# A seven-product FFN matmul group: four products added in one PSUM tile that a copy seeds, in another order, with its banks in a ring of six

## Chip, cores, metric

The kernel runs on one core of one Trainium2 chip. The metric is the time of one execution in microseconds (us), taken on the device; a kernel's time is the median of several runs. One execution is also profiled; its own time and the span of its trace (first to last instruction) are given beside the median.

## What is computed

A decoder trunk of two layers over 512 tokens of width 1024, all in float32. Each layer is FFN, mixer, FFN, so there are four FFNs; the change is in these alone. The reference, cut to what matters:

```python
D_MODEL = 1024; SEQ = 512; DEPTH = 2; D_FF = 2816

def swiglu(h, w_gate, w_up, w_down):
    return (jax.nn.silu(h @ w_gate) * (h @ w_up)) @ w_down

for i in range(DEPTH):
    x = x + 0.5 * swiglu(rmsnorm(x, ffn1_norm[i]), ffn1_w_gate[i], ffn1_w_up[i], ffn1_w_down[i])
    h = rmsnorm(x, mix_norm[i])
    x = x + (gla_mixer(h, ...) if i % 2 == 0 else sb_mixer(h, ...))
    x = x + 0.5 * swiglu(rmsnorm(x, ffn2_norm[i]), ffn2_w_gate[i], ffn2_w_up[i], ffn2_w_down[i])
return rmsnorm(x, final_norm)
```

## The kernel before, in words

**Tiles and precision.** Activations lie feature-major: tiles of 128 features by 512 tokens. Every float32 operand is cut into a high part `h` and a low part `l` (tile type float32r), and each product is three matmuls, high by high, low by high and high by low. The weights are cut by `Entry.split`: ScalarE (ACT) casts the raw weights to `wh` (L133), VectorE (DVE) subtracts to get `wl` (L134). The raw weights come from DRAM in chunks of 1024 rows by 256 columns (`raw`, two buffers), the down weights in chunks `rawd` of 512 KB. A pair `wh`, `wl` has four buffers, the pair for down weights one, so ACT's cast of down weights has to wait until TensorE (PE) has done with the down product before it.

**The feed.** The work on PE is a queue of entries; each has weights to be cut and a body that issues matmuls. `Feed.start` cuts the weights of up to three entries ahead and loads those of six.

**The seven-product group** (`seven`, the function that is changed). From chunk 3 on for the gate matrix and chunk 2 on for the up matrix, one chunk of 256 columns against the 512 tokens is done as a 2 by 2 block product with seven block products in place of eight (Winograd's form of Strassen's scheme). The weights' blocks are A11, A12, A22 and the sums S1 to S4 of blocks (`sums_12`, `sums_34`, two DVE instructions each); the activations' blocks are `half` (plain) and `t_half` (sums, made once in an FFN). A block product, `prod`, is 4 steps of 3 matmuls of 256 columns, 12 matmuls (L528). Each FFN has 17 such groups, 8 for gate and 9 for up, 68 in all; here they are numbered 0 to 16 in an FFN, the even ones up, the odd ones gate. A group has two entries, `body_1` with four products and `body_2` with three.

The group has three PSUM tiles, `w`, `z` and `q`. Before the change a product that has to be added to several outputs is put in a PSUM region of its own, and the sums are made by DVE outside PSUM: A11 goes to `w` and is copied to an SBUF tile `u2` by ACT (L563); S2 goes to `z`, and DVE adds it to `u2` (L539); S1 goes to `q` and ACT copies it to `c5` (L570); A12 is accumulated in `w`, whose sum is the first output quarter (`left`: a SiLU by ACT, L543, in a gate group, a multiplication by DVE, L545, in an up group). S3 goes to the second half of `z`; DVE adds `u2` and then `c5` (L539, L583). S4 is accumulated in `q`, DVE adds `u2`. A22 goes to the second half of `w`; DVE adds it. `rest` applies SiLU (L549) or the gate (L552), and `close` cuts an up group's result into `hh`, `hl` for the down product.

**The down products** (`down`) stand between the groups. One gives a tile `ps_d`, 12 matmuls of 512 columns (6 in the group of one chunk), and DVE adds it to the residual `x` (L308).

**PSUM.** There are eight banks, under four tags of 2, 3, 2 and 1 buffers; `psum(name)` without a tag takes the next of a ring of eight, for groups, down products and the rest alike.

**What sets the order.** Each engine runs its instructions in the order of its own stream and waits on semaphores. The framework that builds the program lays out each stream and may move an instruction ahead of another one of the code; the built streams are what is shown below.

## Time and profile before

| | us |
|---|---|
| median of 3 runs (lowest to highest) | 1829.39 (1829.24 to 1830.08) |
| the profiled execution | 1829.62 |
| span of its trace | 1827.8 |
| DVE busy | 1454.1 |
| ACT busy | 935.9 |

The profile's page gives the busy time of each engine, the span in 40 slices, the chain of work that ended last and groups of equal instructions with the idle time before them. A timeline row is: start, duration (both us), engine, line, operation, output<-inputs, shape; in brackets the idle time of the engine before it and what ended it. The end of a matmul is modelled, so a product is timed from its first matmul's start to the next product's first. DVE and ACT instructions overlap by some 0.1 us in these rows: the next one may start before the last has ended.

### The profile page before, as it was taken

The page shows a single profiled execution, that of the slowest core. Times are in us where ns is not written, and L with a number is a line of the kernel's source. Part 1 is how long each engine was busy: PE and PEld are TensorE (multiplying, and loading weights), DVE is VectorE, ACT ScalarE, POOL GpSimd, SP SyncE. Part 2 cuts the span into 40 slices and gives each one's busy share as a digit, 9 for nine tenths or more (in the row PEclk, how much of TensorE's full clock was granted, in tenths as well). Part 3 has the DMA queues.
Part 4 walks back from the last instruction along what each step waited for, and adds up shares of the span by engine and source line. Part 5 has one row for each costly group of instructions (what it writes and reads, how often), then busy time and mean ns, then how long its engine had stood idle before and what let it go on. Part 6 is the DMA issues. An engine that isn't in the chain of part 4 may idle for free.

```text
span 1827.8 us, 28865 instructions
## 1 busy us (share of the span) xinstructions
PE 1794.6 (98%) x11790; PEld 1642.5 (90%) x11790; DVE 1454.1 (80%) x2311; ACT 935.9 (51%) x1450; POOL 7.3 (0%) x17
## 2 busy tenths in 40 slices
PE   7999999999999999999999999999999999999998
PEld 6899999889988899999989999999888788999997
DVE  5987878775776988887889878777878769888785
ACT  5544444543664544444464444445888855444344
POOL 0000000100000000000000000000000000000000
PEclk9999999999999999999999999999999999999999
DMA  5333332322123333333234233223222222333321
GB/s 162 101 119 104 106 126 82 113 70 70 47 70 102 107 115 105 104 116 105 81 109 134 86 122 105 92 94 104 70 64 64 67 95 93 127 105 104 117 92 69
DMA packets 177511, 179.01 MB, mean 98 GB/s; under 512 B 4034, under 2 KB 167924, under 8 KB 177380
## 3 DMA queue, kind: packets, MB, share of 16 engines
q1 hardware_dynamic: 176192, 175.13, 29.7%
q8 instruction: 92, 1.51, 0.3%
q0 software_dynamic: 512, 0.99, 0.2%
q10 hardware_dynamic: 676, 1.07, 0.2%
q14 instruction: 39, 0.32, 0.1%
HBM read 175.11 MB, written 2.10 MB: 97 GB/s over the span
## 4 chain that ended last, share of the span: by engine, by line
PE 82%; DVE 10%; ACT 4%; DMA 3%; issue 1%; SPq 0%; ACTq 0%; DVEq 0%
PE ps_d L62 24%; PE ps_w L528 14%; PE ps_f L62 12%; PE ps_z L528 9%; PE ps_q L528 9%; PE ps_t L62 4%; PE ps_b L62 3%; DVE wl L134 2%; PE ps_S L62 1%; DMA raw<-in_ffn_w_up_dram 1%; PE ps_bt L62 1%; ACT wh L133 1%; PE ps_oT L1141 1%; PE ps_z L1079 1%; ACT l L439 1%
## 5 line engine op out<-in xcount | busy, mean ns | idle before, releaser
L134 DVE TENSOR_TENSOR wl<-raw,wh 128x1024 fp32r<-128x1024 f32 x244 | 261.9, 1073 | 68.2 <-ACT wh L133 67.2
L133 ACT CAST wh<-raw 128x1024 fp32r<-128x1024 f32 x244 | 225.4, 927 | 120.9 <-PE ps_f L62 42.0
L62 PE MATMUL ps_d<-hh,wh 128*128 128x512 f32 x672 | 255.0, 379 | 0.0
L62 PE MATMUL ps_d<-hl,wh 128*128 128x512 f32 x672 | 254.8, 379 | 0.0
L62 PE MATMUL ps_d<-hh,wl 128*128 128x512 f32 x672 | 254.8, 379 | 0.0
L133 ACT CAST wh<-s 128x1024 fp32r<-128x1024 f32 x136 | 142.3, 1046 | 131.9 <-PE ps_q L528 76.8
L62 PE MATMUL ps_f<-xh,wh 128*128 128x512 f32 x448 | 177.2, 396 | 5.2 <-ACT wh L133 3.7
L134 DVE TENSOR_TENSOR wl<-s,wh 128x1024 fp32r<-128x1024 f32 x136 | 166.0, 1222 | 17.8 <-ACT wh L133 16.5
L308 DVE SCALAR_TENSOR_TENSOR x<-ps_d,x 128x512 f32<-128x512 f32 x184 | 125.2, 689 | 64.5 <-PE ps_d L62 64.5
L62 PE MATMUL ps_f<-xh,wl 128*128 128x512 f32 x448 | 170.8, 381 | 0.5 <-DVE wl L134 0.5
L62 PE MATMUL ps_f<-xl,wh 128*128 128x512 f32 x448 | 170.5, 381 | 0.0
L133 ACT CAST wh<-rawd 128x1024 fp32r<-128x1024 f32 x84 | 88.0, 1048 | 136.1 <-PE ps_d L62 115.1
L528 PE MATMUL ps_z<-th,wh 128*128 128x256 f32 x544 | 150.2, 276 | 3.1 <-DVE u L539 3.1
L528 PE MATMUL ps_w<-nh,wl 128*128 128x256 f32 x544 | 149.7, 275 | 0.0
L528 PE MATMUL ps_z<-tl,wh 128*128 128x256 f32 x544 | 149.7, 275 | 0.0
L528 PE MATMUL ps_w<-nl,wh 128*128 128x256 f32 x544 | 149.7, 275 | 0.0
L528 PE MATMUL ps_z<-th,wl 128*128 128x256 f32 x544 | 149.7, 275 | 0.0
L528 PE MATMUL ps_w<-nh,wh 128*128 128x256 f32 x544 | 149.6, 275 | 0.0
L62 PEld LDWEIGHTS ps_d<-hl,wh 128*128 128x128 f32 x672 | 127.1, 189 | 17.9
L62 PEld LDWEIGHTS ps_d<-hh,wh 128*128 128x128 f32 x672 | 127.3, 189 | 16.5
L62 PEld LDWEIGHTS ps_d<-hh,wl 128*128 128x128 f32 x672 | 127.3, 189 | 16.4
L134 DVE TENSOR_TENSOR wl<-rawd,wh 128x1024 fp32r<-128x1024 f32 x84 | 102.8, 1224 | 38.3 <-ACT wh L133 38.0
(250 smaller groups left out, 4707.1 us busy)
## 6 DMA issues: line engine op xcount, KB each, us to landing
raw<-in_ffn_w_gate_dram SPq DMA_DIRECT2D x43, 1024.0 KB, 5.2
raw<-in_ffn_w_up_dram SPq DMA_DIRECT2D x43, 1024.0 KB, 5.2
rawd<-in_ffn_w_down_dram SPq DMA_DIRECT2D x84, 512.0 KB, 3.4
raw<-in_gla_w_in_dram SPq DMA_DIRECT2D x12, 1024.0 KB, 5.2
raw<-in_sb_w_in_dram SPq DMA_DIRECT2D x16, 512.0 KB, 3.7
raw<-in_gla_w_out_dram SPq DMA_DIRECT2D x4, 1024.0 KB, 4.9
raw<-in_sb_w_in_dram SPq DMA_DIRECT2D x4, 1024.0 KB, 5.0
raw<-in_sb_w_out_dram SPq DMA_DIRECT2D x4, 1024.0 KB, 4.9
```

Of the source, the lines that this page charges most:

```text
L62: st["pe"] = nc.tensor.matmul(ps, l, r, start=first, stop=last).ins
L133: nc.scalar.copy(h, r).ins,
L134: nc.vector.tensor_tensor(out=l, in0=r, in1=h.bitcast(F32), op=ALU.subtract).ins,
L308: nc.vector.scalar_tensor_tensor(out=x, in0=back_by(ps, 4), scalar=0.5, in1=x, op0=ALU.mult, op1=ALU.add)
L439: st["last"] = nc.scalar.activation(o, i, fn, **kw).ins
L528: nc.tensor.matmul(pairs(o), l_, r_, start=first and j + n == 0, stop=j == 3 and n == 2, skip_group_check=True)
L1079: nc.tensor.matmul(o_, l_, r_, start=first, stop=last, skip_group_check=True)
L1141: nc.tensor.matmul(po[e * 64 : e * 64 + 64, j * P : T], self.v[j][:, c : c + 64], self.wt[p, e][bk][:, c0 : c0 + n], start=j == 0, stop=j ...
```

## The change

In a group, ACT copies A11's result from `w` into `z`, PSUM to PSUM. S2, S3 and A22 are then accumulated onto it in `z`, and between them the running sum is read out: after S2 by an ACT copy to `u2`, after S3 by a DVE addition of `c5` straight into the output tile, after A22 by `left`. The order of the products is A11 S1 S2 A12 S3 S4 A22 (before: A11 S2 S1 A12 S3 S4 A22). In an up group `left` now runs twice on 256 columns in place of one multiplication of 512. The three tiles use the first 256 columns of their banks alone, and the groups take them from a ring of six banks of their own (not the two of tag "a"), while the other PSUM tiles keep their ring of eight, which the groups no longer move on.

```diff
-    turn_ = [0]
+    turn_ = [0, 0]
     def psum(name, tag=None):
-        if tag is None:
+        if tag == "s":
+            tag = "zzztto"[turn_[1] % 6]
+            turn_[1] += 1
+        elif tag is None:
...
             def body_1(W):
-                v["w"], v["z"], v["q"] = psum("ps_w"), psum("ps_z"), psum("ps_q")
-                w, z, q = (v[n][:, 0:H] for n in "wzq")
+                v["w"], v["z"], v["q"] = (psum(n, "s")[:, 0:H] for n in ("ps_w", "ps_z", "ps_q"))
+                w, z, q = (v[n] for n in "wzq")
                 v["o"] = self.tp.tile([P, T], F32, tag="t", name="o0")
                 prod(w, ax, 0, half(0, 0))
-                v["u2"] = part("u2")
-                nc.scalar.copy(v["u2"], w)
-                yield
-                prod(z, s, 4, lambda j: self.t_half(1, j))
-                add(v["u2"], z, v["u2"])
+                nc.scalar.copy(z, w)
                 yield
                 prod(q, s, 0, lambda j: self.t_half(0, j))
                 v["c5"] = part("c5")
                 nc.scalar.copy(v["c5"], q)
                 yield
+                prod(z, s, 4, lambda j: self.t_half(1, j), first=False)
+                v["u2"] = part("u2")
+                nc.scalar.copy(v["u2"], z)
+                yield
                 prod(w, ax, 4, half(4, 0), first=False)
                 left(v["o"], w)
                 yield
             def body_2(W):
-                q, y = v["q"][:, 0:H], v["z"][:, H:T]
+                q, z = v["q"], v["z"]
-                prod(y, s, 0, lambda j: self.t_half(2, j))
-                u3 = o1[:, 0:H]
-                add(u3, y, v["u2"])
-                nc.vector.tensor_tensor(out=o1[:, H:T], in0=u3, in1=v["c5"], op=ALU.add)
+                prod(z, s, 0, lambda j: self.t_half(2, j), first=False)
+                add(o1[:, H:T], z, v["c5"])
                 yield
                 prod(q, s, 4, half(4, 1), first=False)
                 add(o0[:, H:T], q, v["u2"])
                 rest(o0, H)
                 yield
-                o = v["w"][:, H:T]
-                prod(o, a22, 0, lambda j: self.t_half(3, j))
-                add(o1[:, 0:H], o, u3)
-                rest(o1, 0)
+                prod(z, a22, 0, lambda j: self.t_half(3, j), first=False)
+                left(o1, z)
+                rest(o1, H)
                 yield
```

The built streams at three places follow; lines of the changed kernel are 3 higher than before up to L558. The first place is group 6 of the first FFN, an up group, on PE, where product S4 ends and A22 begins. Before:

```order
L528 MATMUL ps_q_1747<-nh_502,wl_1704 128x256
L528 MATMUL ps_q_1747<-nl_503,wh_1703 128x256
L528 MATMUL ps_w_1745<-th_553,wh_1707 128x256 [waits DVE_49]
L528 MATMUL ps_w_1745<-th_553,wl_1708 128x256
L528 MATMUL ps_w_1745<-tl_554,wh_1707 128x256
```

After, at the same place:

```order
L531 MATMUL ps_q_1741<-nh_502,wl_1698 128x256
L531 MATMUL ps_q_1741<-nl_503,wh_1697 128x256
L65 MATMUL ps_d_1871<-hh_839,wh_1733 128x512 [waits DVE_49]
L65 MATMUL ps_d_1871<-hh_839,wl_1734 128x512
L531 MATMUL ps_z_1740<-th_553,wh_1701 128x256 [waits DVE_49]
L531 MATMUL ps_z_1740<-th_553,wl_1702 128x256
L531 MATMUL ps_z_1740<-tl_554,wh_1701 128x256
```

Two matmuls of the down product that follows have moved ahead of A22, and A22 now writes `z`. In a gate group with a down product behind it one matmul has moved; where another group follows at once, two or three of that group's first matmuls have. In 20 of the 68 groups, moreover, the first matmul of the next down product (or group) has moved to between A11 and S1.

The second place is the same group on DVE, from the cut of the next weights (`wl`) to the sums of this group. Before:

```order
L134 TENSOR_TENSOR wl_1804<-raw_1655,wh_1803 128x1024 [waits PE_49,Activation_49]
L545 TENSOR_TENSOR o0_1748<-ps_w_1745,o0_1589 128x256 [waits PE_49]
L134 TENSOR_TENSOR wl_1811<-s12_1807,wh_1810 128x1024 [waits Activation_49]
L539 TENSOR_TENSOR o1_1816<-ps_z_1746,u2_1761 128x256 [waits PE_49]
L539 TENSOR_TENSOR o0_1748<-ps_q_1747,u2_1761 128x256 [waits PE_49]
L583 TENSOR_TENSOR o1_1816<-o1_1816,c5_1788 128x256 [waits DVE_49]
```

After:

```order
L137 TENSOR_TENSOR wl_1798<-raw_1650,wh_1797 128x1024 [waits PE_49,Activation_49]
L548 TENSOR_TENSOR o0_1742<-ps_w_1739,o0_1584 128x256 [waits PE_49]
L137 TENSOR_TENSOR wl_1805<-s12_1801,wh_1804 128x1024 [waits Activation_49]
L542 TENSOR_TENSOR o1_1810<-ps_z_1740,c5_1768 128x256 [waits PE_49]
L542 TENSOR_TENSOR o0_1742<-ps_q_1741,u2_1782 128x256 [waits PE_49]
```

The read of `z` after S3 keeps its place behind the two cuts; of the three additions around it one is gone.

The third place is ACT in group 5 of the first FFN, a gate group, from the cast of the down weights on. Before:

```order
L133 CAST wh_1580<-rawd_1417 128x1024 [waits DMAHW7_49,PE_49,Activation_49]
L563 COPY u2_1602<-ps_w_1586 128x256 [waits PE_49]
L570 COPY c5_1629<-ps_q_1588 128x256 [waits PE_49,Activation_49]
L133 CAST wh_1644<-raw_1488 128x1024 [waits DMAHW0_49,Activation_49]
L543 ACTIVATE o0_1589<-ps_w_1586 128x256 [waits PE_49]
L133 CAST wh_1651<-s12_1648 128x1024
```

After:

```order
L136 CAST wh_1575<-rawd_1413 128x1024 [waits DMAHW7_49,PE_49]
L565 COPY ps_z_1582<-ps_w_1581 128x256 [waits PE_49]
L569 COPY c5_1610<-ps_q_1583 128x256 [waits PE_49,Activation_49]
L573 COPY u2_1624<-ps_z_1582 128x256 [waits PE_49,Activation_49]
L136 CAST wh_1639<-raw_1484 128x1024 [waits DMAHW0_49]
L546 ACTIVATE o0_1584<-ps_w_1581 128x256 [waits PE_49]
L136 CAST wh_1646<-s12_1643 128x1024
```

One copy is added, and the last of the three stands behind the third product (S2) as `c5` stood behind the third product (S1) before; what follows is the same.

## The prediction

> **What bounds the kernel now.** I read the page first, then who waits for whom on PE, then the timeline of two groups.

> ```profile
> span 1827.8 us, 28865 instructions
> PE 1794.6 (98%) x11790; PEld 1642.5 (90%) x11790; DVE 1454.1 (80%) x2311; ACT 935.9 (51%) x1450; POOL 7.3 (0%) x17
> PEclk9999999999999999999999999999999999999999
> ```

> PE is busy for 1794.6 of 1827.8 us, and the change takes no matmul away. So it can only gain what PE idles now. In the view of waits, filtered to PE, the seven-product groups (the rows with `ps_z L528` and `ps_w L528`) have this:

> ```profile
> PE ps_z L528 <- DVE u L539: 3.1, 5, 1.4
> PE ps_w L528 <- DVE o L545: 0.7, 2, 0.3
> ```

> That is 3.8 us in seven waits, all in the first groups of an FFN and in one disturbed by a late load. Nearly all groups run without a gap, which the chain of work that ended last shows for one up group (group 6 of the third FFN):

> ```profile
> 1042.13 1.34 PE ps_z L528 x12
> 1043.47 1.34 PE ps_q L528 x12
> 1044.81 1.34 PE ps_w L528 x12
> 1046.15 5.18 PE ps_d L62 x24
> ```

> A block product takes **1.34 us**, a matmul of a down product 5.18 / 24 = 0.216 us. So a new wait that is covered by one product has 1.34 us in which the other engine must see the end, take its turn, finish and tell PE.

> **What the change saves, and why that is worth little.** Per group three DVE additions go (five before, two now) and an up group gets one more multiplication; ACT gets one copy. By the groups of instructions:

> ```profile
> L539 DVE TENSOR_TENSOR o<-ps_z,u 128x256 f32<-128x256 f32 x68 | 28.5, 419 | 0.0
> L563 ACT COPY u<-ps_w 128x256 f32<-128x256 f32 x68 | 25.3, 372 | 18.5 <-PE ps_w L528 18.5
> L570 ACT COPY c<-ps_q 128x256 f32<-128x256 f32 x68 | 25.3, 372 | 141.6 <-PE ps_q L528 141.6
> L1228 ACT ACTIVATE ps_bt<-x 128x512 f32<-128x512 f32 x8 | 4.8, 602 | 8.2 <-DVE x L1223 8.2
> ```

> DVE loses 68 x 3 x 0.419 - 36 x 0.42 = some 70 us of 1454, ACT gains 68 x 0.372 = 25 us of 936. Neither is the bound, so both count as nothing in themselves: PE's 98% hides them. But the first row matters. The read of `z` after S3 never has idle time before it (0.0 for all 68): DVE always gets to it late, out of a queue. Before the change no matmul waits for that read. After it, **A22 does**, since it accumulates into the same `z`, and only S4 lies between.

> **The new waits, one by one.** In each group PE now waits (1) in S2 for ACT's copy of `w` into `z`, with S1 as cover, (2) in S3 for ACT's copy of `z` to `u2`, with A12 as cover, (3) in A22 for DVE's addition, with S4 and the moved matmuls as cover. The cost of a wait that is not covered comes from one that the trace has (group 1 of the first FFN, DVE's row, then PE's):

> ```profile
> 91.74 0.42 DVE L539 TENSOR_TENSOR u<-ps_z,u 128x256 f32<-128x256 f32 x1
> ...
> 91.56 0.28 PE L528 MATMUL ps_w<-nl,wh 128*128 128x256 f32 x1
> 92.22 0.38 PE L528 MATMUL ps_z<-th,wh 128*128 128x256 f32 x1 [0.39 <-DVE u L539]
> 92.43 0.28 PE L528 MATMUL ps_z<-th,wl 128*128 128x256 f32 x1
> ```

> The addition ended at 92.16; the second matmul came at 92.43, so the first counts as begun one step of 0.11 earlier, at 92.32. PE goes on **0.16 us** after the end of what it waited for.

> (1) and (2): the gate group after the one above, ACT's rows, and the first matmul of its second product:

> ```profile
> 1051.41 1.05 ACT L133 CAST wh<-rawd 128x1024 fp32r<-128x1024 f32 x1 [1.23 <-PE ps_d L62]
> 1052.71 0.37 ACT L563 COPY u<-ps_w 128x256 f32<-128x256 f32 x1 [0.25 <-PE ps_w L528]
> ...
> 1052.51 0.28 PE L528 MATMUL ps_z<-th,wh 128*128 128x256 f32 x1
> ```

> The copy of `w` ends at 1053.08, PE could go on at 1053.24, and S2 as third product is due at 1052.51 + 1.34 = 1053.85: 0.61 us to spare. The copy now goes to PSUM. The trace has no copy from PSUM to PSUM; the nearest rows are ACT's write of 512 columns to PSUM, 602 ns (L1228 above), and 372 ns for 256 columns out of PSUM. Between those ends the copy costs 0.37 to 0.60, and even the upper one leaves 0.38 us. I take 0.37 and no wait. The copy of `z` after S2 stands where that of `c5` stands now and has the same margin. Nothing of length is queued between the three copies on ACT. So (1) and (2) cost nothing.

> (3), the up group. ACT's, DVE's and PE's rows:

> ```profile
> 1040.88 0.37 ACT L570 COPY c<-ps_q 128x256 f32<-128x256 f32 x1 [2.36 <-PE ps_q L528]
> 1041.15 1.05 ACT L133 CAST wh<-raw 128x1024 fp32r<-128x1024 f32 x1
> 1042.17 1.05 ACT L133 CAST wh<-s 128x1024 fp32r<-128x1024 f32 x1
> ...
> 1042.23 1.23 DVE L134 TENSOR_TENSOR wl<-raw,wh 128x1024 fp32r<-128x1024 f32 x1 [0.21 <-ACT wh L133]
> 1043.38 0.42 DVE L545 TENSOR_TENSOR o<-ps_w,o 128x256 f32<-128x256 f32 x1
> 1043.71 1.22 DVE L134 TENSOR_TENSOR wl<-s,wh 128x1024 fp32r<-128x1024 f32 x1
> 1044.84 0.42 DVE L539 TENSOR_TENSOR o<-ps_z,u 128x256 f32<-128x256 f32 x1
> ...
> 1044.65 0.28 PE L528 MATMUL ps_w<-th,wh 128*128 128x256 f32 x1
> ```

> This is a chain: the third product ends, ACT copies, casts, DVE cuts, multiplies, cuts, adds. DVE even waits 0.21 us for ACT at its head, so a DVE with fewer additions doesn't start it sooner, and the order after the change has the same chain with `u2` for `c5`. The addition ends at 1045.26, PE could go on at 1045.42. A22 is due at 1044.65, and with two down matmuls moved ahead of it at 1044.65 + 2 x 0.216 = 1045.08. **0.34 us** are left as a wait.

> (3), the gate group:

> ```profile
> 1055.71 1.05 ACT L133 CAST wh<-raw 128x1024 fp32r<-128x1024 f32 x1
> 1056.73 0.39 ACT L543 ACTIVATE o<-ps_w 128x256 f32<-128x256 f32 x1
> 1057.01 1.04 ACT L133 CAST wh<-s 128x1024 fp32r<-128x1024 f32 x1
> ...
> 1058.12 1.22 DVE L134 TENSOR_TENSOR wl<-s,wh 128x1024 fp32r<-128x1024 f32 x1
> 1059.25 0.42 DVE L539 TENSOR_TENSOR o<-ps_z,u 128x256 f32<-128x256 f32 x1
> ...
> 1059.21 0.28 PE L528 MATMUL ps_w<-th,wh 128*128 128x256 f32 x1
> ```

> The second cut starts 0.07 us after the cast at 1057.01 ends, so here too ACT's chain decides. The addition ends at 1059.67, PE goes on at 1059.83; A22 with one moved matmul is due at 1059.21 + 0.216 = 1059.43: **0.40 us**.

> Behind the waiting A22 on PE stand the rest of the down product and all later groups; DVE's additions to `x` and ACT's cast of down weights wait for those. So each wait moves everything, and since the chain starts anew at each group's third product, it doesn't shrink from group to group.

> Groups 2 to 16 of an FFN are like these two: 4 x 8 = 32 up groups x 0.34 = 10.9 us; 4 x 7 = 28 gate groups x 0.40 = 11.2 us.

> **Groups 0 and 1.** There DVE is behind by more. First and third FFN, DVE's addition and A22 in group 0:

> ```profile
> 86.54 0.42 DVE L539 TENSOR_TENSOR o<-ps_z,u 128x256 f32<-128x256 f32 x1
> 84.97 0.28 PE L528 MATMUL ps_w<-th,wh 128*128 128x256 f32 x1
> ...
> 982.12 0.42 DVE L539 TENSOR_TENSOR o<-ps_z,u 128x256 f32<-128x256 f32 x1
> 981.13 0.38 PE L528 MATMUL ps_w<-th,wh 128*128 128x256 f32 x1 [0.33 <-DVE o L545]
> ```

> First FFN: 86.96 + 0.16 = 87.12 against 84.97 + 3 x 0.11 (three matmuls of group 1 moved ahead) = 85.30, so 1.8 us; I take the same for the second. Third: less the one addition (0.33, the step to the next row on DVE) 82.21 + 0.16 in place of 81.13, so 1.24 later, less the three moved matmuls 0.9; the same in the fourth. Group 1 then waits some 0.4 in each FFN, and what it waits now (about 0.6 in the first two) goes. Sum: 2 x (1.8 + 0.4 - 0.6) + 2 x (0.9 + 0.4) = 5.8 us.

> **The matmuls moved up behind A11** (20 groups) use the cast that ends at 1052.46 above and stand at 1052.51: they wait until 1052.62, 0.11 each, 2.2 us. The bounds are 0 (the cast was early) and the whole cast row, 1.05; the row itself stands nearest.

> **The ring of six.** A group can get a bank that a down product has just left, or the reverse. The tightest is `q` on the bank of the last down tile: that is needed one product after the group's start, and DVE's addition to `x` has long room. I cost it at nothing; with the cover gone it is one DVE row, under 0.7 us, in a quarter of the groups, 12 us at most.

> **Sum.** 10.9 + 11.2 + 5.8 + 2.2 = 30 us on the profiled execution's 1829.62 us (span 1827.8, 1.8 around it; the median shown is 1829.39, 0.2 less): **1859.5 us**.

> **Rivals.**
> *A22 doesn't wait* (not slower). The addition is late because DVE is loaded, and with three additions fewer it comes in time. The point from which this decides: it must end 0.34 (up) and 0.40 us (gate) earlier than now. For it speaks that one addition of 0.33 ahead of it goes; against it that both chains start at ACT, with DVE waiting. Then the 3.8 us of waits go as well, with some 0.1 of restart at each of seven: 1829.6 - 4.5 = 1825 us.
> *A copy comes late too.* If ACT is held up, by a cast ahead of a copy, beyond the 0.61 us, S2 or S3 waits as well. At one cast of 1.05 us that is 1.05 - 0.61 = 0.44 in each group, 68 x 0.44 = 30 us more: 1889 us. The order has no cast between the copies in the steady groups, which speaks against it.
> *The clock falls.* [...] The windows that have many short idles now:

> ```profile
> 1260.00:1480.00 220.00, 217.02 (x1333) 180.09 (x1332) 168.53 (x247) 169.51 (x333) 0.00 (x0) 1.00 0.23 70
> ```

> PE idles 3 us in these 220, in pieces, and the granted clock is 1.00. The forecast is 0.4 us in 9.4 to 14.6. If one product after each wait ran at half the clock, it would be 68 x 1.34 = 91 us more, 1951 us. [...] The window above speaks against it for idles of this length.

> **Chances and range.** Forecast 0.82, no wait 0.08, late copies 0.08, clock 0.02. The forecast's own bounds: without the 2.2, and with the 0.16 taken as 0.06 (the step from the DVE row to the matmul's recorded start), 60 x 0.10 + 2.2 = 8 less; with half of the 5.8 us of the first two groups 3 less again; with the ring's 12 us more. The range is **1848 to 1872 us**, which leaves out the rivals. Within 0.2% (3.7 us, about what a measurement of this kernel can tell from no change): 0.04, of which 0.03 from the rival without a wait and 0.01 from a forecast whose waits nearly vanish; faster by more: 0.05, the rest of that rival; slower: 0.91.

> **What would show it.** In the changed kernel's waits on PE: a row of `ps_z` waiting for DVE `o`, near 68 times, in all some 20 to 28 us, longest about 1.8, and none of length for ACT's copies. ACT's copies should take 0.37 us. PE's clock row should stay at 9. In the group of 12 matmuls of A22 the product before it should look 0.3 to 0.4 us longer. The prediction is wrong if DVE's read of `z` comes earlier than now relative to S3's end, or if PE's new idle time stands before S2 or S3.

## The result, and the profile after

| | before | after |
|---|---|---|
| median, us (lowest to highest) | 1829.32 (1829.24 to 1830.08), 4 runs | 1860.22 (1859.45 to 1861.27), 4 runs |
| ratio after/before, 95% interval | | 1.0168 (1.0156 to 1.0180) |
| span of the profiled execution, us | 1827.8 | 1858.9 |
| chain of work that ended last | PE 82%, DVE 10%, ACT 4% | PE 64%, DVE 21%, ACT 10% |

The changed kernel takes 30.9 us more, for the same 11790 matmuls and 168 fewer instructions on DVE. From its page, the head, the engines and the group of matmuls that A22 belongs to (a group's row ends with the idle time ahead of it and what ended most of that):

```profile
span 1858.9 us, 28644 instructions
...
PE 1814.6 (98%) x11790; PEld 1642.6 (88%) x11790; DVE 1394.6 (75%) x2143; ACT 965.7 (52%) x1552; POOL 7.3 (0%) x17
...
L531 PE MATMUL ps_z<-th,wh 128*128 128x256 f32 x816 | 231.8, 284 | 15.0 <-DVE o L542 9.6
```

L542 is the addition that reads `z` after S3. PE's share of the span is 98% as before, because a recorded matmul lasts 0.28 us while the next starts 0.11 us after it: a hole of 0.2 us lies under the recorded end of the matmul ahead and isn't counted as idle. The view of waits shows how much is hidden in that way. Filtered to PE's matmuls it has six waits, filtered to the loads of their weights it has 68 (us in total, times, longest):

```profile
PE ps_z L531 <- DVE o L542: 9.6, 6, 2.1
```

```profile
PEld ps_z L531 <- DVE o L542: 37.1, 68, 2.3
```

68 is one in each seven-product group. What a wait costs PE is read from the starts of its matmuls: from the one ahead of A22 to A22's first, and from that to the second, less the usual 0.112 us each (0.216 after a matmul of 512 columns). The timeline of an up group in the third FFN, DVE first, then PE (start, duration, engine, line, operation):

```profile
1060.69 0.42 DVE L548 TENSOR_TENSOR o<-ps_w,o 128x256 f32<-128x256 f32 x1
1061.02 1.22 DVE L137 TENSOR_TENSOR wl<-s,wh 128x1024 fp32r<-128x1024 f32 x1
1062.15 0.42 DVE L542 TENSOR_TENSOR o<-ps_z,c 128x256 f32<-128x256 f32 x1
```

```profile
1060.51 0.28 PE L531 MATMUL ps_z<-tl,wh 128*128 128x256 f32 x1
...
1061.96 0.38 PE L65 MATMUL ps_d<-hh,wl 128*128 128x512 f32 x1
1062.18 0.38 PE L65 MATMUL ps_d<-hl,wh 128*128 128x512 f32 x1
1062.63 0.38 PE L531 MATMUL ps_z<-th,wh 128*128 128x256 f32 x1
1062.84 0.28 PE L531 MATMUL ps_z<-th,wl 128*128 128x256 f32 x1
```

S3's last matmul starts at 1060.51 and ends at 1060.79. DVE reads `z` only at 1062.15, behind a cut of the next weights, and is done at 1062.57. A22 follows 0.06 us later, at 1062.63, where it was due at 1062.18 + 0.216 = 1062.40, and its second matmul comes 0.21 us after its first in place of 0.11: 0.23 + 0.10 = 0.33 us are lost. No bracket marks it, since the matmul ahead is drawn until 1062.56.

Measured like this, A22 waits in all 68 groups, 32.9 us in all. Before, A22 waited in two of them, 1.2 us.

### The profile page after: what moved, and what is told of

Same layout as the page of the kernel before. It is cut to its first block, busy times and chain, and to the rows that moved or that the text cites. A ratio compares the mean times of both kernels' runs of the same rounds, so it can differ in the third digit from the quotient of the medians.

```text
span 1858.9 us, 28644 instructions
## 1 busy us (share of the span) xinstructions
PE 1814.6 (98%) x11790; PEld 1642.6 (88%) x11790; DVE 1394.6 (75%) x2143; ACT 965.7 (52%) x1552; POOL 7.3 (0%) x17
## 3 DMA queue, kind: packets, MB, share of 16 engines
q8 instruction: 92, 1.51, 0.3%
## 4 chain that ended last, share of the span: by engine, by line
PE 64%; DVE 21%; ACT 10%; DMA 3%; issue 2%; SPq 0%; ACTq 0%; DVEq 0%
PE ps_d L65 22%; PE ps_z L531 10%; DVE wl L137 9%; PE ps_f L65 8%; ACT wh L136 6%; PE ps_q L531 5%; PE ps_w L531 4%; PE ps_t L65 4%; PE ps_b L65 3%; DMA raw<-in_ffn_w_up_dram 1%; PE ps_S L65 1%; DVE o L542 1%; DVE ts L623 1%; PE ps_bt L65 1%; ACT u L573 1%
## 5 line engine op out<-in xcount | busy, mean ns | idle before, releaser
L531 PE MATMUL ps_z<-th,wh 128*128 128x256 f32 x816 | 231.8, 284 | 15.0 <-DVE o L542 9.6
L531 PE MATMUL ps_z<-tl,wh 128*128 128x256 f32 x816 | 224.9, 276 | 0.0
L531 PE MATMUL ps_z<-th,wl 128*128 128x256 f32 x816 | 224.8, 276 | 0.0
L531 PEld LDWEIGHTS ps_z<-th,wh 128*128 128x128 f32 x816 | 156.6, 192 | 37.6 <-DVE o L542 37.1
L531 PEld LDWEIGHTS ps_z<-tl,wh 128*128 128x128 f32 x816 | 157.1, 192 | 0.0
L531 PEld LDWEIGHTS ps_z<-th,wl 128*128 128x128 f32 x816 | 156.8, 192 | 0.0
```

What stands on the lines that cost most here:

```text
L531: nc.tensor.matmul(pairs(o), l_, r_, start=first and j + n == 0, stop=j == 3 and n == 2, skip_group_check=True)
```

## The experiments

The theory is the prediction's: PE waits in A22 for DVE's read of `z`, which is late because it is queued behind a cut; the rest of the change costs little. The rivals put the time on the ring of six, on the seed and on three products in one bank, or on the order of the products. All diffs are against the changed kernel, except where another is named.

**1. A22 waits for ScalarE's copy.**

```diff
-                add(o1[:, H:T], z, v["c5"])
+                nc.scalar.copy(o1[:, H:T], z)
+                add(o1[:, H:T], o1[:, H:T], v["c5"])
```

> After S3 ScalarE copies z to SBUF, and VectorE's add takes it from there; A22 waits for ScalarE's copy only. Order, seed and ring are those of the change. Theory (A22 waits for a read of z that is late because it is queued on VectorE behind the cut of weights): ScalarE's copy ends about 0.45 us after S3's end, S4 covers 1.34, so the 0.33 and 0.37 us before A22 go in all groups, the 1.8 to 2.3 of groups 0 too; ps_z loses nearly all of its 39 us of lost time, 1822 to 1831 us. Rival 1 (S2, S3 and A22 in one accumulation cost time by themselves, or the ring does): the lost time stays or moves to another product of the group, 1855 to 1863 us. Rival 2 (ScalarE, with 25 us more, makes the casts late): a part comes back at ps_q and ps_w, 1835 to 1850 us.

Measured: 1833.66 us (11 runs), with the kernel before at 1830.77 on that chip; ratio 1.0018 (1.0010 to 1.0027). The loss shrinks from 1.7% to 0.2%. An up group of this kernel, ACT, DVE and PE:

```profile
1046.44 0.37 ACT L584 COPY o<-ps_z 128x256 f32<-128x256 f32 x1 [0.29 <-PE ps_z L531]
```

```profile
1046.64 1.22 DVE L137 TENSOR_TENSOR wl<-s,wh 128x1024 fp32r<-128x1024 f32 x1
1047.78 0.42 DVE L542 TENSOR_TENSOR o<-o,c 128x256 f32<-128x256 f32 x1
```

```profile
1047.47 0.28 PE L531 MATMUL ps_q<-nl,wh 128*128 128x256 f32 x1
1047.58 0.28 PE L531 MATMUL ps_z<-th,wh 128*128 128x256 f32 x1
1047.69 0.28 PE L531 MATMUL ps_z<-th,wl 128*128 128x256 f32 x1
```

DVE's addition is as late as ever: it starts at 1047.78, after A22 has begun. But it reads SBUF now, and PE doesn't wait for it. ACT's copy ends at 1046.81, 0.77 us before A22 is due, and A22 starts 0.11 us after the matmul ahead. In all 68 groups the wait before A22 is gone. Seed, shared bank, order and ring are still there, so none of them is what cost the 31 us.

The time is 2.7 us above my upper end. Some 1.4 us of that is the chip (the kernel before takes 1830.77 us on it, 1829.32 on the first one); for the rest there is a reason that I hadn't seen. In the waits of the weight loads stands a new one:

```profile
PEld ps_z L531 <- ACT ps_z L565: 4.3, 5, 1.1
```

By the matmuls' starts S2 waits 0.9 to 1.15 us for the seeding copy in group 1 of each FFN, 4.1 us in all (the fifth wait is in the last group of the fourth FFN). In the changed kernel S2 doesn't wait there; I take it that the 1.8 to 2.4 us that A22 waits in group 0 leave ACT time. Experiment 6 takes this up.

**2. The ring alone undone.**

```diff
-                v["w"], v["z"], v["q"] = (psum(n, "s")[:, 0:H] for n in ("ps_w", "ps_z", "ps_q"))
+                v["w"], v["z"], v["q"] = (psum(n)[:, 0:H] for n in ("ps_w", "ps_z", "ps_q"))
```

> The changed kernel with the banks of before: the three tiles of a group from the ring of eight. Theory (the ring costs nothing): within 2 us of the changed kernel's 1860.2, and the same 0.33 and 0.37 us before A22. Rival (the ring of six hands out banks that are read late): 12 us less or more of it gone, 1848 us or below.

Measured: 1865.32 us (4 runs), ratio 1.0186 (1.0172 to 1.0200), on the chip of experiment 1. That is above my 2 us around 1860.2, but the changed kernel itself took 1862.91 in one run on another chip (experiment 7), a ratio of 1.0184. The same wait is there, of the same length:

```profile
PEld ps_z L531 <- DVE o L542: 36.2, 68, 3.0
```

By the matmuls' starts A22 loses 0.33 us in the up groups and 0.37 in the gate groups, as with the ring of six. The ring doesn't bring the loss. The profiled execution was the fastest of the four (1861.05 us, the others 1865.18 to 1866.04), so its trace doesn't show what the others lost; whether the ring is worth up to some 3 us either way stays open.

**3. A22 in its own bank again.** The order, the seed, and S2 and S3 added on it stay. A22 goes to the second half of the bank of `w`, ACT copies `z` out after S3, and the banks are fixed.

```diff
-                v["w"], v["z"], v["q"] = (psum(n, "s")[:, 0:H] for n in ("ps_w", "ps_z", "ps_q"))
-                w, z, q = (v[n] for n in "wzq")
+                v["w"], v["z"], v["q"] = psum("ps_w", "t"), psum("ps_z", "z"), psum("ps_q", "a")
+                w, z, q = (v[n][:, 0:H] for n in "wzq")
...
-                q, z = v["q"], v["z"]
+                q, z, o = v["q"][:, 0:H], v["z"][:, 0:H], v["w"][:, H:T]
...
-                add(o1[:, H:T], z, v["c5"])
+                nc.scalar.copy(o1[:, 0:H], z)
+                add(o1[:, H:T], o1[:, 0:H], v["c5"])
...
-                prod(z, a22, 0, lambda j: self.t_half(3, j), first=False)
-                left(o1, z)
-                rest(o1, H)
+                prod(o, a22, 0, lambda j: self.t_half(3, j))
+                add(o1[:, 0:H], o, o1[:, 0:H])
+                rest(o1, 0)
```

> The changed kernel's order, its seeding copy and S2 and S3 added on it, but A22 in the second half of w's bank, as before, and summed by VectorE; z is read by a copy of ScalarE. The banks are fixed (w, z, q from the rings of t, z, a). Theory (only A22's wait for the read of z costs): the lost time before A22 goes, S2 and S3 wait for nothing; 1822 to 1832 us, with one VectorE addition of 0.42 us more in each group hidden. Rival (the seed, or three products in a row on one bank, or the order costs): 1850 us or more.

Measured: 1833.72 us (10 runs), ratio 1.0016 (1.0007 to 1.0025). Of 68 waits before A22 four are left, in group 0 of each FFN, for another reader: `o` here lies in the second half of the bank of `w`, and L548 is the read of `w`.

```profile
PEld ps_w L531 <- DVE o L548: 4.1, 4, 1.3
PEld ps_d L65 <- DVE o L542: 3.5, 3, 1.8
```

The steady groups lose nothing. So two products accumulated on a seed cost nothing; it takes the fourth, over a tile that is read late. The time is 1.7 us above my range, of which some 1.4 us is the chip, as in experiment 1. What makes the rest isn't shown: the waits in group 0 (4.4 us by the matmuls' starts) stand against the 5.6 us that S3 and A22 waited in the kernel before, and the wait of `ps_d` is new.

**4. One read of `z` more.**

```diff
+                add(o1[:, 0:H], z, v["c5"])
                 add(o1[:, H:T], z, v["c5"])
```

> VectorE reads z twice after S3 (a second addition of the same two operands, into a half that is written again later), so A22 waits for one read more, 0.33 us on VectorE. The order on PE changes with it: 3 down matmuls of 0.216 stand ahead of A22 in the groups where the changed kernel has 2 (up) or 1 (gate), and where those are matmuls of the next A11, 5 of 0.112 in place of 2. Theory (VectorE's read of z sets when A22 starts, moved matmuls only cover): the wait is 0.33 + 0.33 - 0.22 = about 0.45 us in up groups, 0.37 + 0.33 - 0.43 = about 0.27 in gate groups, and as before where the next A11's matmuls cover; in sum no change, 1857 to 1865 us. Rival (something else that lies fixed in time holds A22, and not VectorE's read): the moved matmuls shorten the wait to 0.11 in up groups and nothing in gate groups, some 16 us less, 1844 us.

Measured: 1862.42 us (4 runs), ratio 1.0178 (1.0164 to 1.0192), and group by group what the theory said: groups 0 aside, 0.45 us in the up groups (0.73 in one) and 0.27 in the gate groups (0.36 in the two of each FFN where the next A11 covers). One up group, DVE and PE; DVE's two reads are one row:

```profile
1034.65 0.75 DVE L542 TENSOR_TENSOR o<-ps_z,c 128x256 f32<-128x256 f32 x2
```

```profile
1034.89 0.38 PE L65 MATMUL ps_d<-hl,wh 128*128 128x512 f32 x1
1035.45 0.38 PE L531 MATMUL ps_z<-th,wh 128*128 128x256 f32 x1 [0.18 <-DVE o L542]
1035.66 0.28 PE L531 MATMUL ps_z<-th,wl 128*128 128x256 f32 x1
```

The second read ends at 1035.40 and A22 starts 0.05 us later, with three down matmuls moved ahead of it. DVE's read sets the time, and the moved matmuls only fill it; in sum nothing changes, which is why the total alone would have told nothing here.

**5. The cut behind the read.** VectorE's work on the next weights, the sums as well as the cuts, gets an order: after the addition that reads `z`.

```diff
...
+            def body():
+                run = e.body(e.W)
+                next(run)
+                with tc.issue_after(st["read"]):
+                    self.ahead(i)
+                yield
+                yield from run
...
-                add(o1[:, H:T], z, v["c5"])
+                st["read"] = nc.vector.tensor_tensor(out=o1[:, H:T], in0=z, in1=v["c5"], op=ALU.add).ins
```

> The changed kernel with one order added: VectorE's cuts of the next weights are queued behind its addition that reads z, no longer ahead of it. Arithmetic, operations and banks are those of the change; no matmul stands between S4 and A22. Theory (the read is late because it is queued behind a cut that waits for ScalarE's cast): the addition ends about 0.6 us after S3's end, S4 covers it, and the 0.33 and 0.37 us before A22 go; 1824 to 1836 us, if the later cuts don't hold A11 or S1. Rival 1 (the read takes its time whatever stands ahead of it, or something else than VectorE's read holds A22): 1858 us or more, as the matmuls moved ahead as cover are gone too. Rival 2 (the cuts are then late): the lost time moves to ps_w and ps_q, 1840 to 1870 us.

Measured: 1885.01 us (4 runs), ratio 1.0300 (1.0278 to 1.0323), slower than the theory and rival 2 allowed, as rival 1 would have it by the time alone. Yet the read comes when the theory says, here in an up group on DVE and PE:

```profile
1039.89 0.42 DVE L600 TENSOR_TENSOR o<-ps_z,c 128x256 f32<-128x256 f32 x1 [0.92 <-PE ps_z L547]
1040.23 1.22 DVE L138 TENSOR_TENSOR wl<-raw,wh 128x1024 fp32r<-128x1024 f32 x1
```

```profile
1040.85 0.28 PE L547 MATMUL ps_q<-nl,wh 128*128 128x256 f32 x1
1040.96 0.28 PE L547 MATMUL ps_z<-th,wh 128*128 128x256 f32 x1
```

DVE now waits for PE (0.92 us of idle time), reads at 1039.89 and is done 0.65 us before A22 starts on time. Of 68 waits before A22 five are left, 4.0 us in all. What rival 2 named came in their place, and was dearer than I allowed:

```profile
PEld ps_q L547 <- DVE wl L138: 10.9, 8, 1.4
PEld ps_q L547 <- ACT wh L137: 10.7, 16, 0.9
PEld ps_w L547 <- ACT wh L137: 7.9, 4, 2.4
```

So the work on the next weights ahead of the read was what made the read late, and it stood there for a reason: held back, it makes the next group's weights late, ACT's casts among them. A part of the time goes with the clock: the granted clock has a mean of 0.993 over this execution and of 0.997 over that of the changed kernel, where it fell once (last section).

**6. The seeding copy ahead of two casts.** Diff against experiment 1.

```diff
+            self.held = []
...
+                if len(self.held) < 2:
+                    self.held.append((o, group))
+                    return
                 self.close(o, group)
...
-                nc.scalar.copy(z, w)
+                seed = nc.scalar.copy(z, w).ins
+                if len(self.held) == 2:
+                    with tc.issue_after(seed):
+                        for h in self.held:
+                            self.close(*h)
+                    self.held.append(None)
```

> The kernel whose VectorE addition takes z from ScalarE's copy (e1_act_read), with one order more: in group 1 of each FFN the two casts of group 0's results stand behind the seeding copy on ScalarE, no longer ahead of it. Theory (S2 waited 0.8 to 1.05 us in that group because the copy stood behind a cast that waits for VectorE): the four waits before S2, 4.2 us in all, go, and 1.4 us before S1 are left: 1828 to 1831 us where the kernel before takes 1830.8, no difference that can be told. Rival (the copy is late by itself, or the down product then waits for the later casts): no gain, 1833 us or more.

Measured: 1830.39 us (11 runs), with the kernel before at 1829.31; ratio 1.0004 (0.9995 to 1.0013). The four waits of S2 in groups 1 are gone; A22 waits there in three FFNs instead, 0.9 us in all. In the third FFN the copy now has its place ahead of the cast:

```profile
984.35 0.36 ACT L569 COPY ps_z<-ps_w 128x256 f32<-128x256 f32 x1 [0.72 <-PE ps_w L532]
984.95 0.62 ACT L623 CAST hh<-o 128x512 fp32r<-128x512 f32 x1 [0.25 <-DVE o L556]
```

This is the change's form without its loss (and with one copy by ACT more in each group), and it is no faster than the kernel before. Its VectorE is busy for 1392.5 us, 62 less than before, and PE for 1797.4 of a span of 1829.4.

**7. The changed kernel once more**, for the clock (last section).

> The changed kernel once more, unchanged, for the place of the clock's fall. Theory 1 (the granted clock is set anew on a grid of 3.413 us, by how long PE stood idle within one step of the grid, and falls for the next step where that was 2.2 us or more): the grid lies elsewhere against the kernel this time, and each wait of 2 to 2.3 us in groups 0 shows a fall if it lies whole within one step and none if it is cut in two. Rival (a wait of some length by itself, or this place of the program): the fall is again in group 0 of the third FFN, or at every wait over 2.1 us. 1857 to 1863 us either way.

Measured: 1862.91 us, one run; A22 again loses 32.9 us in 68 groups.

## Why the prediction was right

- **The sum.** 1859.5 us was forecast, 1860.22 measured. The terms, from the matmuls' starts in the changed kernel's trace:

| term | forecast | measured |
|---|---|---|
| 32 up groups | 10.9 (0.34 each) | 10.9 (0.33 each; 0.61 in one) |
| 28 gate groups | 11.2 (0.40 each) | 12.0 (0.37 each; 2.03 in one) |
| groups 0 and 1, net of what waited there before | 5.8 | 6.1 |
| matmuls moved up behind A11 | 2.2 (0.11 each) | 1.5 (0.06 to 0.10 each) |
| a late load before, gone from its place | not in the sum | -1.7 |
| the clock's fall | a rival | 1.6 |
| sum | 30.1 | 30.4 (span: 31.1) |

The mechanism and the sizes of the steady groups hold. That the total comes within a microsecond is in part luck: the clock's 1.6 us were not in the sum, and the late loads, 1.7 us in one gate group here and 1.7 before, cancel.

- **Groups 0 and 1** are 8.5 + 1.5 us, less 3.9 that S3 and A22 waited there before. In group 0 A22 waits 1.79, 2.35, 2.21 and 2.18 us in the four FFNs. The prediction had 1.8 in the first, and 0.9 in the third and fourth over what was there; S3 and A22 waited 1.39 and 1.36 us there, so 0.82 us are new in each. Only the second was off, by 0.55 us: it was taken to be like the first. Its own row of before says more:

```profile
653.96 0.42 DVE L539 TENSOR_TENSOR o<-ps_z,u 128x256 f32<-128x256 f32 x1
```

The addition ends at 654.38, and A22 stood at 652.05. With the restart of 0.16 and the three moved matmuls (0.33) this gives 2.16 us.

- **The matmuls moved up** to between A11 and S1 are in 26 groups by the trace, not in 20. In 20 of the 26 they cost 0.06 to 0.10 us, in the other six nothing.
- **What is saved** was too high: DVE's busy time fell by 59.5 us (1454.1 to 1394.6) and not by some 70, since the rows that were summed overlap. ACT's rose by 29.8 us and not by 25, since in a gate group, too, one instruction of 512 columns (the SiLU) became two of 256. As neither engine is the bound, the sum didn't use these.
- **The restart** of 0.16 us after the releaser's end holds: 0.06 to the first matmul and 0.10 more to the second in the group shown.
- **The late load** in the gate group with 2.03 us (DVE idle for 2.68 us ahead of it, for gate weights) has its like in the kernel before, at S3 of a group in the first FFN (1.68 us), and the two about cancel. Experiment 7 has it in the same gate group again (1.80 us), experiments 2 and 4 haven't; whether the change has a part in where it falls isn't shown.
- **Waits (1) and (2), for ACT's copies**, cost next to nothing in the changed kernel: S2 loses 0.36 us in one group of 68, S3 nothing. The copy from PSUM to PSUM, not in the trace of before, took 358 ns, slightly less than the one to SBUF (372) that it was priced by:

```profile
L565 ACT COPY ps_z<-ps_w 128x256 f32<-128x256 f32 x68 | 24.4, 358 | 18.0 <-PE ps_w L531 17.7
```

- **The ring of six at nothing**: experiment 2 bears it out for the waits in its trace, and to within some 3 us for the time.
- **What it would show.** The row of 68 waits came, though among the weight loads and not among the matmuls, and with 37.1 us, beyond the 20 to 28 given; that row counts idle time of the weight loads, more than the 32.9 us that the matmuls lost.
- **The rivals.** "A22 doesn't wait" fell: three additions fewer on DVE didn't bring the read forward; by experiment 5 what stands ahead of it decides. "A copy comes late" is true of one place, group 1, and showed only when the wait in group 0 was taken away (experiment 1). "The clock falls" didn't happen as the rival had it, with a product at half the clock after each wait (91 us): no run shows that term. The granted clock fell once, to 0.50 for 3.41 us, behind a long wait in a group 0, at 1.6 us.

## What to carry to other kernels

An accumulator that takes one more product must have been read by then, so ask in which queue its last read stands, and what stands ahead of it; a read that nobody waited for may always have been late. Moving that one read to the engine that is idle at that point was worth 27 us here; holding back the work ahead of it cost 24. And 60 us off an engine that isn't the bound gave no time at all, even with the new wait removed.

## What was unexpected in the hardware

```profile
992.98:996.39 3.41, 1.46 (x13) 1.27 (x12) 3.41 (x7) 1.04 (x1) 0.00 (x0) 1.00 0.00 0
996.39:999.80 3.41, 3.41 (x18) 3.41 (x18) 3.00 (x6) 1.24 (x2) 0.00 (x0) 0.50 0.23 64
...
658.47:661.89 3.42, 1.77 (x15) 1.77 (x16) 3.42 (x7) 1.07 (x3) 0.00 (x0) 1.00 0.03 5
661.89:665.30 3.41, 3.41 (x32) 3.38 (x31) 2.54 (x5) 1.83 (x4) 0.00 (x0) 1.00 0.56 176
```

PE was busy for 1.46 of 3.41 us, and the next 3.41 us ran at 0.50: matmuls 0.21 us apart in place of 0.11, some 16 of them, 1.6 us. The wait in the second FFN was even longer (2.35 against 2.21 us), but the grid of steps cut it, so that 1.77 us of its step were busy, and the clock stayed at 1.00. The same kernel again, experiment 7, with the grid elsewhere:

```profile
658.12:661.53 3.41, 1.53 (x14) 1.33 (x13) 3.41 (x8) 1.20 (x2) 0.00 (x0) 1.00 0.02 5
661.53:664.94 3.41, 3.41 (x18) 3.32 (x17) 2.50 (x4) 1.75 (x4) 0.00 (x0) 0.50 0.31 104
996.03:999.45 3.42, 1.63 (x14) 1.63 (x15) 3.42 (x7) 1.15 (x2) 0.00 (x0) 1.00 0.00 0
999.45:1002.86 3.41, 3.41 (x33) 3.41 (x33) 2.68 (x5) 1.87 (x4) 0.00 (x0) 1.00 0.54 151
```

Now the second FFN falls and the third doesn't (and the fourth falls, with 1.45 us busy). Of these five steps the three with PE busy for 1.45, 1.46 and 1.53 us were followed by one at 0.50, and the two with 1.63 and 1.77 us by one at 1.00, as was a step with 1.81 us in the kernel before (from 368.62). They give no sharp bound: a step of the changed kernel with 1.51 us, near its end (from 1849.73), was followed by one at 1.00 too. By these rows neither the place nor the length of a wait decides alone (2.21 us brought a fall, 2.35 us none); how much of it lay in one step went with the fall in the five shown. The 2.2 us of experiment 7's theory were too high for the idle time of a step: in the three that were followed by 0.50 it was 1.88 to 1.96 us. The short waits before A22, 0.33 to 0.61 us in the changed kernel, brought no fall there.
